# Second MLP matrix by seven block products per group, with the hidden features kept in memory

## The chip, the cores and the metric

The kernel runs on one core of one Trainium2 chip. The metric is the device time of one execution in microseconds, the median over several runs. TensorE (PE in the profile) multiplies, VectorE (DVE), ScalarE (ACT) and GpSimd (POOL) work on elements, SyncE (SP) issues the transfers.

## The reference

One step of a two-layer backbone over 1024 latent and 256 context tokens, model width 1024. Layer 0 mixes tokens by a gated DeltaNet and windowed attention, layer 1 by a recurrent block; after each mixer comes an MLP with a hidden width of 4096:

```python
def sq_relu_mlp(h, w1, w2):
    return jnp.square(jax.nn.relu(h @ w1)) @ w2
```

Its input is a modulated RMS norm of the residual `x`; its output times a gate (one column for latent, one for context tokens) is added to `x`. All is in float32.

## The kernel before

Everything is kept transposed: features on the 128 partitions, tokens along the free axis, in three token tiles `TT`: two of 512 latent tokens and one of 256 context tokens (the prompt), `ti` = 0, 1, 2. For products of float32 accuracy each operand is split into a rounded part `hi` and a remainder `lo` (type float32r), and three products are summed in PSUM: hi x hi, hi x lo, lo x hi (`gemm_tile`, L466 to L468).

`wload` brings a weight block of 128 x 1024 in two transfers of 256 KB through the raw buffers `wraw` (L451); ScalarE rounds (`whi`, L453), GpSimd or VectorE subtracts (`wlo`, L457). There are four slots of such pairs and four raw buffers.

`ff` is the MLP. The hidden width is cut into 32 chunks of 128. `ff1` computes chunks: 8 input blocks x 3 products for each token tile into a PSUM bank of tag `mm`; ScalarE takes the ReLU (L498) and the rounded square (L499), VectorE the exact square (L501), GpSimd the remainder (L502), into `hidh` and `hidl` (three buffers each). `ff2` multiplies two chunks by their rows of the second matrix: for each of 8 output blocks `o` and each token tile, 2 x 3 products (L518 to L520) into a bank of tag `w`, and VectorE adds bank x gate to the residual tile (L521). There are four banks of each tag. The two alternate, chunk pair by chunk pair, so a chunk lives in SBUF only.

In the last pair the order is token tile by token tile, and `after(o, ti)` is called behind each accumulation. In layer 0 this feeds the next norm (class `Norm`, driven by `norm_steps`): a square on ScalarE for each `o` (L396), its sums over the partitions on TensorE (L332), then per token tile `stat` (sums, L403, power, diagonal rows) and `apply` (L418 to L427), which writes the next `hhi` and `hlo`. What is left over for the last token tile is run inside the first projection of the recurrent mixer (`project` in `mix1`), whose softplus ends at L859 and whose gates multiply at L813. In layer 1 `after` sends finished blocks to the output (L673). Scratch of the norms comes from the MLP's own buffers (`ff_scratch`).

In layer 0's mixer, before the MLP, the memory tensor `dn` carries blocks from one stage (L1444, L1495) to another (L1559).

The Tile framework sets the order on each engine's queue, starting from program order, with a model of the instructions' durations, and derives all waits; buffers with one tag rotate, `bufs` of them. All transfers are issued by SP's queue. `hhi`, `hlo` are the tags `hh0` to `hh2` and `hl0` to `hl2` of the pool `hp`.

## Time and profile before

| | us |
|---|---|
| median of 3 runs | 3313.18 |
| lowest, highest | 3306.25, 3314.08 |
| the profiled execution | 3308.6 |
| its span | 3306.8 |

The span goes from the first to the last recorded instruction. Durations of instructions are from the one profiled execution; matmuls are pipelined, so the recorded durations of neighbours overlap. `PEld` is TensorE's weight load, which runs beside its products. "Idle before" is time for which an engine stood still before an instruction, with what ended it behind the arrow.

### The profile page before, as it was taken

Reading aid. Unit: us, or ns where it says so; the run is one execution under the profiler, and the core shown is the slowest. Engines: PE = TensorE matmul, PEld = TensorE weight load, DVE = VectorE, ACT = ScalarE, POOL = GpSimd, SP = SyncE. Lnnn points to the kernel's source line nnn. Section 1 sums busy time; section 2 is a strip of 40 time slices with the busy share of each in tenths; the row PEclk is TensorE's granted clock in tenths of the full one; section 3 lists DMA queues with packets and bytes.
Section 4 is the critical chain, followed back from the end, with each engine's and each line's share of the span. In section 5 each row is a group of like instructions: output and inputs, shape, how many; then the busy total and the mean of one; then the engine's idle time right before and its main releaser. Section 6 shows DMA issues by size and latency. Waiting matters only on the chain.

```text
span 3306.8 us, 50448 instructions
## 1 busy us (share of the span) xinstructions
PE 3150.0 (95%) x20311; PEld 2555.8 (77%) x20311; DVE 1783.5 (54%) x3080; ACT 1117.5 (34%) x2004; POOL 714.3 (22%) x637
## 2 busy tenths in 40 slices
PE   8989966899999999999999999998999999999999
PEld 5867754665568788888888877886778888888888
DVE  5549887667633544444444447778164444444444
ACT  5455523453332321212121236787142121212121
POOL 0000004455432321212121211000142222222220
PEclk9999987999999999999999999999999999999999
DMA  5356777446951011101010121111211111111111
GB/s 201 86 144 171 182 182 207 127 125 212 285 195 33 32 39 32 45 32 45 33 45 32 45 74 41 40 36 43 82 39 45 39 42 36 41 36 40 38 39 70
DMA packets 219272, 273.90 MB, mean 83 GB/s; under 512 B 71578, under 2 KB 125626, under 8 KB 219038
## 3 DMA queue, kind: packets, MB, share of 16 engines
q1 hardware_dynamic: 219038, 270.68, 27.2%
q8 instruction: 159, 2.61, 0.3%
q14 instruction: 75, 0.61, 0.1%
HBM read 223.69 MB, written 46.92 MB: 82 GB/s over the span
## 4 chain that ended last, share of the span: by engine, by line
PE 76%; DVE 8%; DMA 3%; ACT 3%; issue 2%; POOL 1%; SPq 1%; DVEq 0%; ACTq 0%; POOLq 0%
PE ps_mm L466 13%; PE ps_mm L467 13%; PE ps_mm L468 13%; PE ps_w L518 9%; PE ps_w L519 9%; PE ps_w L520 9%; DVE prod L1473 2%; PE ps_ad L300 2%; PE ps_w L1832 1%; PE ps_w L1828 1%; PE ps_w L332 1%; DVE Vinv L1474 1%; DMA adaw<-ada 1%; PE ps_w L1604 1%; PE ps_s L1791 1%
## 5 line engine op out<-in xcount | busy, mean ns | idle before, releaser
L466 PE MATMUL ps_mm<-hhi,whi 128*128 128x512 f32 (+2 forms) x2768 | 991.1, 359 | 21.0 <-ACT hhi L564 13.5
L467 PE MATMUL ps_mm<-hlo,whi 128*128 128x512 f32 (+2 forms) x2768 | 990.1, 358 | 11.0 <-POOL hlo L427 10.8
L468 PE MATMUL ps_mm<-hhi,wlo 128*128 128x512 f32 (+2 forms) x2768 | 987.8, 358 | 0.7 <-POOL wlo L457 0.7
L521 DVE SCALAR_TENSOR_TENSOR x<-ps_w,mod,x 128x512 f32<-128x512 f32 (+1 forms) x768 | 504.1, 660 | 590.9 <-PE ps_w L520 590.9
L466 PEld LDWEIGHTS ps_mm<-hhi,whi 128*128 128x128 f32 (+1 forms) x2768 | 525.8, 190 | 105.2 <-ACT hhi L564 13.9
L467 PEld LDWEIGHTS ps_mm<-hlo,whi 128*128 128x128 f32 (+1 forms) x2768 | 526.0, 190 | 92.9 <-POOL hlo L427 14.3
L468 PEld LDWEIGHTS ps_mm<-hhi,wlo 128*128 128x128 f32 (+1 forms) x2768 | 526.2, 190 | 79.8 <-issue 6.4
L519 PE MATMUL ps_w<-hidl,whi 128*128 128x512 f32 (+1 forms) x1536 | 546.5, 356 | 1.7 <-POOL hidl L502 1.7
L518 PE MATMUL ps_w<-hidh,whi 128*128 128x512 f32 (+1 forms) x1536 | 545.8, 355 | 0.0
L520 PE MATMUL ps_w<-hidh,wlo 128*128 128x512 f32 (+1 forms) x1536 | 543.8, 354 | 0.0
L502 POOL TENSOR_TENSOR hidl<-ffs,hidh 128x512 fp32r<-128x512 f32 (+1 forms) x192 | 226.5, 1180 | 1217.4 <-ACT hidh L499 977.8
L498 ACT ACTIVATE ffr<-ps_mm 128x512 f32<-128x512 f32 (+1 forms) x192 | 100.4, 523 | 902.7 <-PE ps_mm L468 883.6
L453 ACT CAST whi<-wraw 128x512 fp32r<-128x512 f32 x365 | 211.8, 617 | 516.4 <-PE ps_w L519 301.0
L501 DVE TENSOR_TENSOR ffs<-ffr 128x512 f32<-128x512 f32 (+1 forms) x192 | 164.3, 855 | 331.6 <-ACT ffr L498 327.9
L518 PEld LDWEIGHTS ps_w<-hidh,whi 128*128 128x128 f32 x1536 | 290.5, 189 | 45.7 <-issue 1.4
L519 PEld LDWEIGHTS ps_w<-hidl,whi 128*128 128x128 f32 x1536 | 290.4, 189 | 45.0 <-POOL hidl L502 2.5
L520 PEld LDWEIGHTS ps_w<-hidh,wlo 128*128 128x128 f32 x1536 | 289.7, 189 | 41.9 <-issue 0.6
L457 POOL TENSOR_TENSOR wlo<-wraw,whi 128x512 fp32r<-128x512 f32 (+1 forms) x157 | 210.4, 1361 | 259.7 <-ACT whi L453 157.7
L457 DVE TENSOR_TENSOR wlo<-wraw,whi 128x512 fp32r<-128x512 f32 x208 | 147.8, 733 | 90.9 <-ACT whi L453 90.8
L499 ACT ACTIVATE hidh<-ffr 128x512 fp32r<-128x512 f32 (+1 forms) x192 | 107.4, 560 | 5.8
L580 DVE SCALAR_TENSOR_TENSOR x<-ps_mm,mod,x 128x512 f32<-128x512 f32 (+1 forms) x40 | 25.9, 655 | 149.0 <-PE ps_mm L468 138.5
L300 PE MATMUL ps_ad<-adaw,sc 128*32 128x512 f32 x320 | 81.7, 653 | 18.8 <-DMA adaw<-ada 18.8
(377 smaller groups left out, 3272.4 us busy)
## 6 DMA issues: line engine op xcount, KB each, us to landing
wraw<-ff SPq DMA_DIRECT2D x256, 256.0 KB
adaw<-ada SPq DMA_DIRECT2D x80, 512.0 KB
wraw<-w_in SPq DMA_DIRECT2D x76, 256.0 KB
dn<-NI SPq DMA_DIRECT2D x40, 256.0 KB
aw<-ada SPq DMA_DIRECT2D x16, 512.0 KB
wraw<-w_out SPq DMA_DIRECT2D x32, 256.0 KB
dkv<-tok SPq DMA_DIRECT2D x20, 256.0 KB
rtab<-rope SPq DMA_DIRECT2D x10, 512.0 KB
```

What stands on the lines that cost most here:

```text
L300: nc.tensor.matmul(ps[32 * j:32 * j + 32, :], g.sc[:, k, :], w[:, i, :], start=k == 0, stop=k == KC - 1, skip_group_check=True)
L453: nc.scalar.copy(hv[:, o:o + half], raw[:, :half])
L457: e.tensor_tensor(lv[:, o:o + half], raw[:, :half], hv[:, o:o + half], op=ALU.subtract)
L466: nc.tensor.matmul(ps, whi[:, k, :], hhi[:, k, :], start=first and k == k0, stop=False)
L467: nc.tensor.matmul(ps, whi[:, k, :], hlo[:, k, :], start=False, stop=False)
L468: nc.tensor.matmul(ps, wlo[:, k, :], hhi[:, k, :], start=False, stop=last and k == k1 - 1)
L501: nc.vector.tensor_tensor(s[:, :tw], r[:, :tw], r[:, :tw], op=ALU.mult)
L502: nc.gpsimd.tensor_tensor(hl[:, t0:t0 + tw], s[:, :tw], hh[:, t0:t0 + tw], op=ALU.subtract)
L518: nc.tensor.matmul(ps[:, :tw], whi[:, o, :], hh[:, t0:t0 + tw], start=f == 0, stop=False)
L519: nc.tensor.matmul(ps[:, :tw], whi[:, o, :], hl[:, t0:t0 + tw], start=False, stop=False)
L520: nc.tensor.matmul(ps[:, :tw], wlo[:, o, :], hh[:, t0:t0 + tw], start=False, stop=f == 1)
L521: nc.vector.scalar_tensor_tensor(xt[ti][:, o, :], ps[:, :tw], Gt[:, o, cc:cc + 1], xt[ti][:, o, :], op0=ALU.mult, op1=ALU.add)
```

## The change

`ff` now runs the whole first matrix, then the whole second. `ff1` goes through 16 pairs of chunks, squares on VectorE into one float32 tile `hid` per chunk, forms four differences of feature blocks on GpSimd (`tt`), and writes `hid` and `tt` to the memory tensors `Dh` and `Dt`.

`ff2` goes through 8 groups of 4 chunks. For the latent tokens a group is a 2 x 2 block product: output halves of 512 features, contraction halves of 256 (even and odd chunks), token halves of 512. It is computed by Strassen's scheme in Winograd's form: seven block products instead of eight, with sums and differences of weight blocks (GpSimd, on the raw weights) and of feature blocks (read from `Dt`). Each block product is 4 banks x 2 chunks x 3 products; a chain of four of them stays in the same four `mm` banks, and VectorE adds the running bank to the residual after each step where the scheme wants it. The prompt is multiplied in the plain way, from the weight blocks that are there anyway. Raw weights (`ar`), raw features (`br`) and the prompt's split features (`pp`) take over the buffers of `hhi` and `hlo`; feature sets are split by ScalarE and VectorE into `tt` and `hid` in turn, weight sets by ScalarE and GpSimd.

Because the last group finishes the token tiles in the order 0, 2, 1, `norm_steps` and the first `project` take this order. In `mix1` the scratch of the softplus moves into a slice of an `rr` buffer.

The diff; the removed body of `ff` and empty lines are left out (the old body is among the functions printed above):

```diff
@@ -389,8 +389,8 @@
             self.flush(k - 1)
         else:
             self.ps = bank(self.g, SUMTAG)
-        if k == KC - 1 and self.ti == 2:
-            self.sq = self.g.cp.tile([128, self.tw], F32, tag="nsq", name="nsq", bufs=1)
+        if k == KC - 1 and self.late:
+            self.sq = self.g.cp.tile([128, 512], F32, tag="nsq", name="nsq", bufs=1)[:, :self.tw]
         else:
             self.sq = self.al("t%d" % (k % 2))[:, :self.tw]
         self.g.nc.scalar.activation(self.sq, self.x[:, k, :], AF.Square)
...
+NG = NFC // 4
 def ff(g, l, xt, hhi, hlo, Gt, pend, after):
...
+    Dh = g.dp.tile([NFC // 2, 128, 2, T], F32, name=f"dh{l}")
+    Dt = g.dp.tile([NFC // 2, 128, 4, 512], F32, name=f"dt{l}")
+    ff1(g, l, hhi, hlo, pend, Dh, Dt)
+    ff2(g, l, xt, Gt, after, Dh, Dt)
+def ff1(g, l, hhi, hlo, pend, Dh, Dt):
+    nc, pool = g.nc, g.fp
+    for p in range(NFC // 2):
+        ws = [wload(g, g.A["ff1"][l, 2 * p + i], lo_eng=("pool", "dve")[i]) for i in range(2)]
+        hid = [pool.tile([128, T], F32, tag="hid", name="hid", bufs=4) for i in range(2)]
         for ti, (t0, tw) in enumerate(TT):
+            for i in range(2):
                 ps = bank(g, "mm")
+                gemm_tile(g, ps[:, :tw], *ws[i], hhi[ti], hlo[ti])
+                if pend and i:
                     pend.pop(0)()
                 r = pool.tile([128, 512], F32, tag="ffr", name="ffr", bufs=2)
                 nc.scalar.activation(r[:, :tw], ps[:, :tw], AF.Relu)
+                nc.vector.tensor_tensor(hid[i][:, t0:t0 + tw], r[:, :tw], r[:, :tw], op=ALU.mult)
+        t = pool.tile([128, 4, 512], F32, tag="tt", name="tt", bufs=2)
+        (b11, b12), (b21, b22) = [[h[:, 0:512], h[:, 512:1024]] for h in hid]
+        for j, (x, y) in enumerate(((b12, b11), (b22, t[:, 0]), (b22, b12), (b21, t[:, 1]))):
+            nc.gpsimd.tensor_tensor(t[:, j], x, y, op=ALU.subtract)
+        for i in range(2):
+            nc.sync.dma_start(Dh[p, :, i], hid[i])
+        nc.sync.dma_start(Dt[p], t)
+def ff2(g, l, xt, Gt, after, Dh, Dt):
+    nc, pool, src = g.nc, g.fp, g.A["ff2"][l]
+    count = [0]
+    def acc(ps, ti, o):
+        cc, tw = (0, 0, 1)[ti], TT[ti][1]
+        nc.vector.scalar_tensor_tensor(xt[ti][:, o, :], ps[:, :tw], Gt[:, o, cc:cc + 1], xt[ti][:, o, :], op0=ALU.mult, op1=ALU.add)
+    def weights(srcs):
+        w, i = g.wslots[g.nw % len(g.wslots)]
+        g.nw += 1
+        hi, lo = [w.tile([128, KC, 128], F32R, tag=n + str(i), name=n).rearrange("p k c -> p (k c)") for n in ("whi", "wlo")]
+        n = 1024 // len(srcs)
+        for j, s in enumerate(srcs):
+            c = slice(n * j, n * j + n)
+            nc.scalar.copy(hi[:, c], s)
+            nc.gpsimd.tensor_tensor(lo[:, c], s, hi[:, c], op=ALU.subtract)
+        return hi, lo
+    def split(raw, hi, lo):
+        nc.scalar.copy(hi, raw)
+        nc.vector.tensor_tensor(lo, raw, hi, op=ALU.subtract)
+        return hi, lo
+    def three(ps, a, b, first, last):
+        (ah, al), (bh, bl) = a, b
+        nc.tensor.matmul(ps, ah, bh, start=first, stop=False, skip_group_check=True)
+        nc.tensor.matmul(ps, ah, bl, start=False, stop=False, skip_group_check=True)
+        nc.tensor.matmul(ps, al, bh, start=False, stop=last, skip_group_check=True)
+    def product(pss, a, b, m, first):
+        for i in range(2):
+            c, t = slice(512 * i + 128 * m, 512 * i + 128 * m + 128), slice(512 * i, 512 * i + 512)
+            three(pss[m], [v[:, c] for v in a], [v[:, t] for v in b], first and i == 0, i == 1)
+    for gi in range(NG):
+        last, q = gi == NG - 1, gi % 2
+        ar = g.hp.tile([128, 4, 1024], F32, tag=f"hh{q}", name="ar", bufs=1)
+        br = g.hp.tile([128, 4, 1024], F32, tag=f"hl{q}", name="br", bufs=1)
+        pp = g.hp.tile([128, 2, 1024], F32R, tag=("hh2", "hl2")[q], name="pp", bufs=1)
+        nbr = [0]
+        def load_w(b):
+            for i in range(2):
+                nc.sync.dma_start(ar[:, b, 512 * i:512 * i + 512], src[4 * gi + 2 * i + b % 2][:, 512 * (b // 2):512 * (b // 2) + 512])
+        def feats(srcs):
+            raw = br[:, nbr[0] % 4]
+            nbr[0] += 1
+            for i, s in enumerate(srcs):
+                nc.sync.dma_start(raw[:, 512 * i:512 * i + 512], s)
+            count[0] += 1
+            if count[0] % 2:
+                t = pool.tile([128, 2, 1024], F32R, tag="tt", name="bb", bufs=2)
+                return split(raw, t[:, 0], t[:, 1])
+            return split(raw, *[pool.tile([128, 1024], F32R, tag="hid", name="b" + n, bufs=4) for n in "hl"])
+        def block_of(i, ti):
+            return [Dh[2 * gi + j, :, i, 512 * ti:512 * ti + 512] for j in range(2)]
+        def comb(j):
+            return [Dt[2 * gi + i, :, j - 1] for i in range(2)]
+        def prompt(ws, o0):
+            for m in range(4):
+                ps = bank(g, "w")[:, :256]
+                for i in range(2):
+                    for c in range(2):
+                        w = slice(512 * i + 128 * m, 512 * i + 128 * m + 128)
+                        f = 256 * (2 * i + c)
+                        three(ps, [v[:, w] for v in ws[c]], [pp[:, x, f:f + 256] for x in range(2)], i + c == 0, i + c == 2)
+                acc(ps, 2, o0 + m)
+        chain = [bank(g, "mm") for m in range(4)]
+        load_w(0)
+        a11, b11 = weights([ar[:, 0]]), feats(block_of(0, 0))
+        for m in range(4):
+            product(chain, a11, b11, m, True)
+            acc(chain[m], 0, m)
+        load_w(1)
+        a12, b21 = weights([ar[:, 1]]), feats(block_of(1, 0))
+        pss = [None] * 4
+        for m in range(4):
+            pss[m] = bank(g, "w")
+            product(pss, a12, b21, m, True)
+            acc(pss[m], 0, m)
+        praw = br[:, nbr[0] % 4]
+        nbr[0] += 1
+        for i in range(2):
+            nc.sync.dma_start(praw[:, 512 * i:512 * i + 512].rearrange("p (c t) -> p c t", t=256), Dh[2 * gi + i, :, :, 1024:])
+        split(praw, pp[:, 0], pp[:, 1])
+        prompt((a11, a12), 0)
+        load_w(2)
+        load_w(3)
+        s1, s2 = [[wraw(g) for i in range(2)] for _ in range(2)]
+        for i in range(2):
+            c = slice(512 * i, 512 * i + 512)
+            nc.gpsimd.tensor_tensor(s1[i], ar[:, 2, c], ar[:, 3, c], op=ALU.add)
+            nc.gpsimd.tensor_tensor(s2[i], s1[i], ar[:, 0, c], op=ALU.subtract)
+        w, f = weights(s2), feats(comb(2))
+        for m in range(4):
+            product(chain, w, f, m, False)
+            acc(chain[m], 1, m)
+        nc.gpsimd.tensor_tensor(ar[:, 0], ar[:, 0], ar[:, 2], op=ALU.subtract)
+        w, f = weights([ar[:, 0]]), feats(comb(3))
+        for m in range(4):
+            product(chain, w, f, m, False)
+            acc(chain[m], 1, 4 + m)
+        a22, f = weights([ar[:, 3]]), feats(comb(4))
+        for m in range(4):
+            product(chain, a22, f, m, False)
+            acc(chain[m], 0, 4 + m)
+            if last:
+                after(m, 0)
+        prompt((weights([ar[:, 2]]), a22), 4)
+        w, f = weights(s1), feats(comb(1))
+        for m in range(4):
+            pss[m] = bank(g, "mm" if last else "w")
+            product(pss, w, f, m, True)
+            acc(pss[m], 1, 4 + m)
+            if last:
+                after(4 + m, 0)
+        for i in range(2):
+            c = slice(512 * i, 512 * i + 512)
+            nc.gpsimd.tensor_tensor(ar[:, 1, c], ar[:, 1, c], s2[i], op=ALU.subtract)
+        w, f = weights([ar[:, 1]]), feats(block_of(1, 1))
+        for m in range(4):
+            if last:
+                after(2 * m, 2)
+                after(2 * m + 1, 2)
+            product(pss, w, f, m, False)
+            acc(pss[m], 1, m)
+            if last:
+                after(m, 1)
         if last:
+            for m in range(4):
+                after(4 + m, 1)
...
 def ff_scratch(g):
     def al(tag):
         if tag == "dg":
-            return g.fp.tile([128, T], F32R, tag="hidl", name="ndg", bufs=3)
-        return g.fp.tile([128, 512], F32, tag={"t0": "ffr", "t1": "ffs"}[tag], name="n" + tag, bufs=2)
+            return g.fp.tile([128, T], F32R, tag="hid", name="ndg", bufs=4)
+        return g.fp.tile([128, 512], F32, tag={"t0": "ffr", "t1": "tt"}[tag], name="n" + tag, bufs=2)
     return al
-def norm_steps(g, ab, al, stat_at, apply_at):
+def norm_steps(g, ab, al, stat_at, apply_at, seq=(0, 1, 2)):
     n, h = {}, {}
     def after(o, ti, x):
+        i = seq.index(ti)
         if o == 0:
             n[ti] = Norm(g, ti, x, al)
+            n[ti].late = i == 2
         n[ti].square(o)
-        if ti and o == stat_at[ti]:
-            n[ti - 1].stat()
-        if ti and o == apply_at[ti]:
-            if ti == 1:
+        if i and o == stat_at[i]:
+            n[seq[i - 1]].stat()
+        if i and o == apply_at[i]:
+            if i == 1:
                 h["h"] = htiles(g.hp)
-            n[ti - 1].apply(*ab, *h["h"])
+            n[seq[i - 1]].apply(*ab, *h["h"])
     def late(f):
         def run(al=None):
-            n[2].al = al or n[2].al
+            n[seq[2]].al = al or n[seq[2]].al
             f()
         return run
-    left = [late(lambda: n[2].stat()), late(lambda: n[2].apply(*ab, *h["h"]))]
+    left = [late(lambda: n[seq[2]].stat()), late(lambda: n[seq[2]].apply(*ab, *h["h"]))]
     return after, left, h
@@ -674,7 +799,7 @@
         with ExitStack() as e2:
             ff_pools(g, e2, ("fp", "wx"))
-            step, left, h1 = norm_steps(g, ab, ff_scratch(g), {1: 2, 2: 3}, {1: 5, 2: 7})
+            step, left, h1 = norm_steps(g, ab, ff_scratch(g), {1: 2, 2: 3}, {1: 5, 2: 7}, (0, 2, 1))
             def end0(o, ti, x):
                 step(o, ti, x)
@@ -758,7 +883,8 @@
     def project(jobs):
         ws = [wload(g, A["w_in1"][c], lo_eng="dve") for c, _ in jobs]
-        for ti, (t0, tw) in enumerate(TT):
+        for ti in (0, 2, 1) if left else (0, 1, 2):
+            tw = TT[ti][1]
             for (c, evac), (whi, wlo) in zip(jobs, ws):
                 ps = bank(g, "mm")[:, :tw]
                 gemm_tile(g, ps, whi, wlo, hhi[ti], hlo[ti])
@@ -850,10 +976,11 @@
         return KC + c, evac
     project([xjob(0), gjob(0)])
-    sp = pool.tile([128, 16], F32, name="sp")
-    nlam = pool.tile([128, 16], F32, name="nlam")
+    tp = Slices([full("rr", 2)])
+    sp = tp.tile([128, 16], F32)
+    nlam = tp.tile([128, 16], F32)
     nc.vector.tensor_scalar(nlam, g.par["lam"], -1.0, None, op0=ALU.mult)
-    softplus(g, sp, nlam, pool, "lsp")
+    softplus(g, sp, nlam, tp, "lsp")
     m8, p4 = pool.tile([128, 16], F32, name="m8"), pool.tile([128, 16], F32, name="p4")
     nc.vector.tensor_scalar(m8, sp, -8.0, None, op0=ALU.mult)
     nc.vector.tensor_scalar(p4, sp, 4.0, None, op0=ALU.mult)
```

## Rows read from the trace of the kernel before

**Rows 1.** the page: busy us, share, instructions; TensorE and its clock in 40 slices

```profile
PE 3150.0 (95%) x20311; PEld 2555.8 (77%) x20311; DVE 1783.5 (54%) x3080; ACT 1117.5 (34%) x2004; POOL 714.3 (22%) x637
...
PE   8989966899999999999999999998999999999999
...
PEclk9999987999999999999999999999999999999999
```

**Rows 2.** the page: the chain that ended last, shares of the span by line

```profile
PE ps_mm L466 13%; PE ps_mm L467 13%; PE ps_mm L468 13%; PE ps_w L518 9%; PE ps_w L519 9%; PE ps_w L520 9%; DVE prod L1473 2%; PE ps_ad L300 2%; PE ps_w L1832 1%; PE ps_w L1828 1%; PE ps_w L332 1%; DVE Vinv L1474 1%; DMA adaw<-ada 1%; PE ps_w L1604 1%; PE ps_s L1791 1%
```

**Rows 3.** windows, inside the first MLP and in a DMA-heavy stretch before it

```profile
core 0: us, PE busy (x) PEld busy (x) DVE busy (x) ACT busy (x) POOL busy (x), PEclk, DMA share, GB/s
1120.00:1900.00 780.00, 780.00 (x4066) 671.14 (x4065) 331.36 (x480) 149.28 (x282) 175.34 (x143) 1.00 0.12 39
800.00:900.00 100.00, 95.84 (x1343) 55.61 (x1341) 74.13 (x188) 39.20 (x102) 54.73 (x45) 1.00 0.85 246
```

**Rows 4.** groups by form, 1120 to 1900: count, busy, mean ns, idle before

```profile
L518 PE MATMUL ps_w<-hidh,whi 128*128 128x512 f32 x455 | 178.2, 392 | 0.0
...
L521 DVE SCALAR_TENSOR_TENSOR x<-ps_w,mod,x 128x512 f32<-128x512 f32 x227 | 170.1, 750 | 207.5 <-PE ps_w L520 207.5
...
L453 ACT CAST whi<-wraw 128x512 fp32r<-128x512 f32 x114 | 66.1, 617 | 203.9 <-PE ps_w L519 139.8 <-DMA wraw<-ff 38.2 <-PE ps_mm L467 22.8
...
L521 DVE SCALAR_TENSOR_TENSOR x<-ps_w,mod,x 128x256 f32<-128x256 f32 x113 | 54.5, 482 | 53.4 <-PE ps_w L520 53.4
```

**Rows 5.** timeline of TensorE, runs of equal products: start us, us, instruction

```profile
1059.03 0.28 PE L466 MATMUL ps_mm<-hhi,whi 128*128 128x256 f32 x1
...
1062.15 0.28 PE L468 MATMUL ps_mm<-hhi,wlo 128*128 128x256 f32 x1
...
1065.24 0.39 PE L466 MATMUL ps_mm<-hhi,whi 128*128 128x512 f32 x1
...
1067.51 0.39 PE L467 MATMUL ps_mm<-hlo,whi 128*128 128x512 f32 x1
```

**Rows 6.** timeline of VectorE, first MLP

```profile
1317.07 1.28 DVE L457 TENSOR_TENSOR wlo<-wraw,whi 128x512 fp32r<-128x512 f32 x2
...
1338.14 0.75 DVE L521 SCALAR_TENSOR_TENSOR x<-ps_w,mod,x 128x512 f32<-128x512 f32 x1 [2.87 <-PE ps_w L520]
1338.81 1.40 DVE L501 TENSOR_TENSOR ffs<-ffr 128x256 f32<-128x256 f32 x1
```

**Rows 7.** timeline of GpSimd, the same stretch

```profile
1337.37 2.55 POOL L457 TENSOR_TENSOR wlo<-wraw,whi 128x512 fp32r<-128x512 f32 x2 [0.66 <-ACT whi L453]
```

**Rows 8.** weight loads, SP's queue: ns min/median/max, first and last start

```profile
L451 SPq DMA_DIRECT2D wraw<-ff x256: 327/328/914, 987.3 to 3271.2; - x128
```

**Rows 9.** the chain in order of time: a 512 KB load

```profile
753.44 4.90 DMA adaw<-ada
```

**Rows 10.** the memory tensor `dn`: ns min/median/max, first and last start

```profile
L1559 SPq DMA_DIRECT2D XW<-dn x40: 444/476/1499, 475.5 to 875.9; - x40
...
L1495 SPq DMA_DIRECT2D dn<-VB x20: 500/616/801, 337.4 to 555.1; - x20
```

**Rows 11.** timeline of VectorE from the first MLP into the recurrent mixer

```profile
1956.36 0.15 DVE L403 TENSOR_SCALAR nst<-ps_w 128x4 f32<-128x4 f32 x1
...
2008.95 0.17 DVE L859 TENSOR_SCALAR p<-sp 128x16 f32<-128x16 f32 x1
```

**Rows 12.** timeline of TensorE, the same stretch

```profile
1965.06 0.73 PE L466 MATMUL ps_mm<-hhi,whi 128*128 128x512 f32 x2 [0.43 <-ACT hhi L419]
...
2017.76 1.09 PE L813 MATMUL ps_w<-xh,lwhi 128*128 128x512 f32 x4
```

**Rows 13.** windows: ten us of it

```profile
1990.00:2000.00 10.00, 7.56 (x20) 5.69 (x21) 9.64 (x13) 6.42 (x11) 6.19 (x7) 0.66 0.17 52
```

**Rows 14.** timeline of VectorE, the last accumulation

```profile
3303.33 0.48 DVE L521 SCALAR_TENSOR_TENSOR x<-ps_w,mod,x 128x256 f32<-128x256 f32 x1 [0.23 <-PE ps_w L520]
```

More of the change, by code (lines that the diff above doesn't have):

```diff
@@ L526, in ff @@
-    ff1(0, 1)
-    for gi in range(NFC // 2):
-        c0 = 2 * gi
-        if c0 + 2 < NFC:
-            ff1(c0 + 2)
-        ff2(c0)
-        if c0 + 3 < NFC:
-            ff1(c0 + 3)
-        del hid[c0], hid[c0 + 1], w2[c0], w2[c0 + 1]
+                nc.vector.tensor_tensor(hid[i][:, t0:t0 + tw], r[:, :tw], r[:, :tw], op=ALU.mult)
[3 more added lines that the diff above has]
+            nc.gpsimd.tensor_tensor(t[:, j], x, y, op=ALU.subtract)
```

36 lines of the change are left out of this document (removed).

## The prediction

> **What bounds the kernel now.** I read the page's busy shares first: TensorE is busy for 95% of the span, VectorE for 54%, GpSimd for 22% [rows 1]. An average says little over a kernel with two mixers and two MLPs, so next comes the chain that ended last, by line: L466 to L468 (the first MLP matrix and every other dense product that goes through `gemm_tile`) and L518 to L520 (the second MLP matrix) hold 66% of it [rows 2]. Then the stretch in the middle of the first MLP: in 780 us TensorE has no idle time at all and its granted clock is 1.00, while DMA works at 39 GB/s and GpSimd for 175 us [rows 3]. Both MLPs are TensorE-bound to the last instruction. There a matmul that is not issued is time saved, as long as nobody else becomes late.
>
> What is one matmul worth? Not its modelled duration of 392 ns [rows 4], since matmuls overlap; it is the distance of two starts. In a row of 128x512 products ten steps take 2.27 us: 0.227 us each. In a row of 128x256 products 26 steps take 3.12 us: 0.12 us each [rows 5]. So a pair of hidden chunks costs 192 x 0.227 + 96 x 0.12 = 55.1 us for both matrices, half of it, 27.5 us, in the second.
>
> **The matmuls.** Before, 4 hidden chunks take 4 x 8 x 2 x 3 = 192 products 512 wide and 96 products 256 wide in the second matrix. After, a group of 4 chunks takes 7 block products of 4 x 2 x 3 = 24, so 168, and the prompt again 2 x 48 = 96. That is 24 fewer x 8 groups x 2 layers = 384 x 0.227 = **-87.1 us**. A group now lasts 168 x 0.227 + 96 x 0.12 = 49.6 us, a block product 5.45 us. The first matrix keeps its 27.5 us for a pair.
>
> **Who must keep up in 49.6 us.** VectorE: 28 accumulations at 0.750 and 8 at 0.482 [rows 4] make 24.9 us; eight feature sets (seven blocks and the prompt) are split anew, and one of 1024 columns is like two of 512, 1.28 us [rows 6], so 10.2; 35.1 in all. GpSimd: a 1024-wide subtraction is two of 512, 2.55 us [rows 7]. Eight weight sets make 20.4; the sums and differences of weights add another four times 1024 columns, 10.2; 30.6 in all. ScalarE rounds 16 sets of 1024 at about 1.2 (two of 0.617 [rows 4]): 20 us. SP issues 8 weight and 16 feature transfers at 0.33 us [rows 8], 8 us. Memory: 24 x 256 KB is 6.3 MB in 49.6 us, 127 GB/s; in the first matrix, 3.4 MB a pair in 27.5 us, 124 GB/s. The trace carries 246 GB/s in another stage [rows 3]. So each of them fits with a margin, and these edits cost nothing under TensorE's 49.6 us. Buffers give the distance: a feature set's destination comes free three block products before it is needed, a weight slot at least two (11 us), and a chain of load, rounding and remainder is 4.9 (half a megabyte, [rows 9]) + 1.2 + 2.6 = 8.7 us.
>
> **The wait that the change adds.** VectorE and GpSimd do not run as freely side by side as this sum pretends. GpSimd worked from 1337.37 to 1339.92; VectorE's 256-wide product of two SBUF operands that began at 1338.81 took 1.40 us and ended 0.29 us after GpSimd [rows 6, 7]. It waited. The accumulation at 1338.14, one operand in PSUM, took its usual 0.75 in the same time [rows 6]. So the splits wait for GpSimd, the accumulations do not, but they stand behind the splits in VectorE's queue, and TensorE waits for their banks. The Trainium skill, SBUF — State Buffer, section "Who interferes with whom", has it as a rule that speaks against this change: a read and write port pair of SBUF is locked exclusively, for a whole instruction, between GpSimd and VectorE instructions with two SBUF inputs; the trace agrees, with the 1.40 us. By the Trainium skill's rule the lock would be held 30.6 + 10.2 = 40.8 of 49.6 us, which still fits.
>
> Now the price. Bounds for one split's wait: nothing, or one whole GpSimd instruction, 2.55 us. GpSimd is busy 62% of the group, so 0.62 x 1.3 = 0.8 us on average: 6.4 us a group, and VectorE stands at 41.5 of 49.6. A bank is wanted again after three quarters of a product, 4.1 us after its last matmul, and its accumulation needs 0.75: 3.3 us of slack against at most 1.28 + 2.55 = 3.8. Only the worst of 128 splits reach TensorE, with half a microsecond each: I take **+5**, bounds 0 and 20.
>
> **From the first matrix to the second** nothing overlaps any more by two chunk halves. The raw buffers take over `hh0` and `hl0`, which are free after the last pair's first token half, so 48 x 0.227 + 48 x 0.12 = 16.6 us before the first matrix ends, against the 8.7 us chain. Would the read of the features wait for the last write to the same memory tensor? No: the first read of `dn` starts at 475.5 while the last write of that tensor starts far later (its writes at L1495 run to 555.1) [rows 10]; overlap goes by region. **+2** for both layers, bounds 0 and 10.
>
> **The end of layer 0.** The next norm's first half needs all eight squares, and odd ones use the slots of `tt`, which the last feature sets also use; the eighth gets its slot when the block product before the last is done, 5.45 us before TensorE runs out. From the sums to the first product of the next stage the trace has 8.7 us (1956.36 to 1965.06) [rows 11, 12], and I allow 3 us, an estimate from the same stretch, for the square, its sums and their copy ahead of it: 11.7 - 5.5 = 6 us late. Before, prompt products of the last pair filled this; now they are finished earlier. And the clock falls to half (1.2 of 2.4 GHz) for some time after such a gap: in 1990 to 2000, granted 0.66 on average, 20 products took 10 us where 4.5 would do [rows 13]. The second and third parts had such gaps already, and some of the 6 us goes to what TensorE still has to do of the norm. **+6**, bounds 0 (sums hoisted) and 18 (three gaps of 6 us). The recurrent mixer's other edits cost nothing: its token parts change places, and the softplus works in slices of an `rr` buffer, which the gates need; before, it was done at 2009.1 and the first gate product began at 2017.8 [rows 11, 12]. Without those 8.6 us of air it would be late by as much, once.
>
> **The tail.** The last transfer is now 512 KB, not 256; before, 3.0 us lie between the last accumulation's end and the end of the span [rows 14]. The 512 KB of [rows 9] took 4.9. **+2.5**, bounds 0 and 5.
>
> **The sum.** The profiled execution took 3308.6 us (span 3306.8 and 1.8 around it): 3308.6 - 87.1 + 5 + 2 + 6 + 2.5 = 3237. It lies 4.6 us under the median of the runs; I place the time between, at **3239**. All lower bounds together give 3221.5, all upper ones 3274.
>
> **The rivals.** (a) *Part of the gain is eaten by late accumulations.* If the fixed order of the queues does not foresee these waits and each of the 128 splits stalls TensorE for 0.4 us, that is +51, so 3284 (the case reaches from 3274 to 3303). For it: VectorE has 8 us of air in 49.6 by my average. Against: a bank's 3.3 us of slack. 0.12. (b) *VectorE becomes the bound, and the kernel is slower.* If every split waits for a whole GpSimd instruction, a group is 24.9 + 10.2 + 8 x 2.55 = 55.5 us of VectorE, 5.9 more than TensorE has; 16 groups make +94, so 3308.6 - 87.1 + 94 + 10 = 3326. It decides over TensorE from 1.8 us of wait a split, and the kernel is slower from 2.4. It is the lock of the Trainium skill's SBUF — State Buffer, taken at its worst. Against it: GpSimd idles 38% of the time. 0.08. (c) *Memory.* If transfers reached only 110 GB/s, a group would be 57 us; 3308.6 - 87.1 + 16 x 7.6 + 10 = 3353. Nothing in the trace at a high DMA share is that slow. 0.03. (d) *The gain is lost in sum,* (a) at 0.6 us a split: 3308, no change. 0.05.
>
> **Chances.** The forecast, within its bounds of 3221 to 3274, has 0.72. Faster is the forecast and (a): 0.84. Within 0.3%, which is 10 us and about what the runs' own spread can tell: 0.05. Slower, (b) and (c): 0.11. For 8 in 10 the range goes from 3221 into the middle of (a), 3285.
>
> **What would show it.** Right: 2688 products 512 wide in the second matrix in place of 3072; TensorE without idle inside the groups, 49.6 us apart; the first matrix at 27.5 us a pair. The lock: splits well over 1.3 us next to GpSimd's subtractions, and, if (a) or (b), TensorE idle until a VectorE accumulation. The seam at layer 0's end: TensorE idle for some 5 us before the projection, and a granted clock under 1. Wrong: a group well over 49.6 us, or TensorE waiting for weights.

## The result and the profile after

The kernel after the change takes 3234.8 us (median of 4 runs, 3231.9 to 3240.2), the one before 3313.6 on the same chip (4 runs, 3306.3 to 3317.0): a ratio of 0.9767, 95% interval 0.9746 to 0.9788, or 78.8 us. The profiled execution took 3233.9 us, its span 3232.1. The forecast was 3239, its range 3221 to 3285.

The page of after, with the lines that answer to [rows 1]: busy time, then TensorE and its granted clock in 40 slices.

```profile
PE 3060.8 (95%) x19927; PEld 2485.3 (77%) x19927; DVE 1864.1 (58%) x2952; ACT 1209.4 (37%) x1972; POOL 1117.5 (35%) x781
...
PE   8989975889989999999999998999899999999999
...
PEclk9999986999999999999999998999999999999999
```

TensorE lost 89.2 us of busy time and kept its 95%: it is still the bound, and all others got busier (GpSimd from 714 to 1118 us). Windows of after inside the first MLP: the seam between the two matrices, then a stretch of the second matrix (columns as in [rows 3]).

```profile
1520.00:1540.00 20.00, 19.83 (x117) 17.35 (x116) 16.78 (x14) 6.84 (x9) 19.53 (x12) 1.00 0.93 329
1540.00:1560.00 20.00, 17.99 (x93) 15.47 (x94) 17.72 (x21) 8.11 (x10) 19.76 (x11) 1.00 0.64 229
...
1600.00:1650.00 50.00, 50.00 (x268) 43.33 (x268) 37.04 (x45) 16.32 (x18) 33.44 (x19) 1.00 0.39 127
```

In the groups TensorE has no idle time, at a granted clock of 1.00, with VectorE at 37 of 50 us, GpSimd at 33 and DMA at 127 GB/s. The same work stands once in each group, for instance the remainder of the prompt's features; timeline of VectorE in after:

```profile
1616.76 1.64 DVE L541 TENSOR_TENSOR pp<-br,pp 128x1024 fp32r<-128x1024 f32 x1 [0.41 <-ACT pp L540]
...
1815.47 1.65 DVE L541 TENSOR_TENSOR pp<-br,pp 128x1024 fp32r<-128x1024 f32 x1 [0.40 <-ACT pp L540]
```

Four groups take 198.71 us, 49.68 each; the forecast was 49.6. Only the seam is different: there GpSimd is busy for 39.3 of 40 us, and TensorE is missing 2.2. The view of waits of after, TensorE, from the start of layer 0's MLP to the end; its five largest lines:

```profile
PE ps_mm L466 <- ACT hhi L686: 13.5, 2, 13.0
PE ps_mm L466 <- ACT hhi L419: 9.7, 7, 1.6
PE ps_mm L467 <- POOL hlo L427: 8.8, 5, 2.3
PE ps_w L368 <- DVE ndg L361: 6.5, 5, 2.5
PE ps_w L546 <- DVE x L526: 4.6, 2, 2.4
```

The last line is the second matrix: two waits in all (us, times, longest), one at each layer's seam. The others are seams of norms and projections. Before waits there too, but less: the same view of it sums to 38.0 us, this one to 45.5, and waits for the row spread of a norm (L368, 6.5 us) have no line in it. The 13.0 us ahead of layer 1's first projection are in both.

**What a comparison can resolve.** Between before and after, 7 us of span go to a stretch that the change leaves alone. From the first projection after layer 0's mixer (its first product that waits for a remainder on VectorE: 938.81 us in before, 945.89 in after) to the end of the span it is 3306.8 - 938.81 = 2368.0 us before and 3232.1 - 945.89 = 2286.2 after: -81.8 where the spans differ by -74.7. I call this *the stretch from layer 0's projection*, and the experiments are compared in it too.

### The profile page after: what moved, and what is told of

The parts are those of the page before. It is cut to its first block, busy times and chain, and to the rows that moved or that the text cites. A ratio compares the mean times of both kernels' runs of the same rounds, so it can differ in the third digit from the quotient of the medians.

```text
span 3232.1 us, 50272 instructions
## 1 busy us (share of the span) xinstructions
PE 3060.8 (95%) x19927; PEld 2485.3 (77%) x19927; DVE 1864.1 (58%) x2952; ACT 1209.4 (37%) x1972; POOL 1117.5 (35%) x781
## 4 chain that ended last, share of the span: by engine, by line
PE 74%; DVE 8%; DMA 3%; issue 3%; ACT 2%; POOL 2%; SPq 1%; DVEq 0%; POOLq 0%; ACTq 0%
PE ps_mm L467 14%; PE ps_mm L466 14%; PE ps_mm L468 13%; PE ps_w L546 4%; PE ps_w L547 4%; PE ps_w L548 4%; PE ps_mm L547 4%; PE ps_mm L548 4%; PE ps_mm L546 4%; DVE prod L1600 2%; PE ps_ad L300 2%; PE ps_w L1959 1%; DVE Vinv L1601 1%; PE ps_w L1955 1%; PE ps_s L1918 1%
## 5 line engine op out<-in xcount | busy, mean ns | idle before, releaser
L468 PEld LDWEIGHTS ps_mm<-hhi,wlo 128*128 128x128 f32 (+1 forms) x2768 | 526.3, 190 | 81.8 <-issue 6.0
L507 DVE TENSOR_TENSOR hid<-ffr 128x512 f32<-128x512 f32 (+1 forms) x192 | 148.9, 777 | 589.3 <-ACT ffr L506 507.1
L536 POOL TENSOR_TENSOR wlo<-ar,whi 128x1024 fp32r<-128x1024 f32 x96 | 246.7, 2584 | 268.7 <-ACT whi L535 251.2
L526 DVE SCALAR_TENSOR_TENSOR x<-ps_mm,mod,x 128x512 f32<-128x512 f32 x272 | 200.4, 746 | 82.8 <-PE ps_mm L548 82.6
L526 DVE SCALAR_TENSOR_TENSOR x<-ps_w,mod,x 128x512 f32<-128x512 f32 (+1 forms) x304 | 185.6, 632 | 100.7 <-PE ps_w L548 100.5
L511 POOL TENSOR_TENSOR tt<-hid 128x512 f32<-128x512 f32 x64 | 83.3, 1301 | 414.0 <-DVE hid L507 414.0
L453 ACT CAST whi<-wraw 128x512 fp32r<-128x512 f32 (+1 forms) x237 | 136.7, 617 | 197.9 <-PE ps_mm L467 84.1
L535 ACT CAST whi<-ar 128x1024 fp32r<-128x1024 f32 x96 | 98.0, 1051 | 292.6 <-PE ps_w L547 208.3
L546 PE MATMUL ps_w<-pp,whi 128*128 128x256 f32 x512 | 143.6, 283 | 4.6 <-DVE x L526 4.6
L547 PE MATMUL ps_w<-pp,whi 128*128 128x256 f32 x512 | 143.4, 283 | 0.0
L548 PE MATMUL ps_w<-pp,wlo 128*128 128x256 f32 x512 | 141.0, 283 | 0.0
L511 POOL TENSOR_TENSOR tt<-hid,tt 128x512 f32<-128x512 f32 x64 | 85.3, 1333 | 118.2 <-DVE hid L507 118.0
```

Of the source, the lines that this page charges most:

```text
L453: nc.scalar.copy(hv[:, o:o + half], raw[:, :half])
L468: nc.tensor.matmul(ps, wlo[:, k, :], hhi[:, k, :], start=False, stop=last and k == k1 - 1)
L507: nc.vector.tensor_tensor(hid[i][:, t0:t0 + tw], r[:, :tw], r[:, :tw], op=ALU.mult)
L511: nc.gpsimd.tensor_tensor(t[:, j], x, y, op=ALU.subtract)
L526: nc.vector.scalar_tensor_tensor(xt[ti][:, o, :], ps[:, :tw], Gt[:, o, cc:cc + 1], xt[ti][:, o, :], op0=ALU.mult, op1=ALU.add)
L536: nc.gpsimd.tensor_tensor(lo[:, c], s, hi[:, c], op=ALU.subtract)
```

## The experiments

**An eighth product.** In every group a11 x b11 is issued twice into the same banks; the second overwrites the first.

```diff
             product(chain, a11, b11, m, True)
+            product(chain, a11, b11, m, True)
```

> The first block product of each group is issued twice (the second start overwrites the first, so all else is as in the changed kernel): 24 more products of 512 columns in each of 16 groups. Theory (TensorE sets the pace of every group, the gain is the product that is left out): 384 x 0.227 = 87 us more, 3322 us, a little over the kernel before. Rival (the gain comes from running the two matrices one after the other, with fewer accumulations and one split each, and TensorE has air): less than half of it, under 3280.

Measured: 3324.9 us, ratio to before 1.0028 (1.0017 to 1.0039), 90.1 us over after. The 384 products cost what their distance says, 87.1, and a little more. TensorE sets the time, and the products are the gain: with the eighth one the changed kernel is 0.28% slower than the one before, so the rest of the change wins nothing by itself.

**Six products.** s2 x c2 is left out, its sets are still loaded and split.

```diff
         w, f = weights(s2), feats(comb(2))
         for m in range(4):
-            product(chain, w, f, m, False)
```

> The products of the second weight combination are left out (24 in each group; its weights and features are still loaded and split, its accumulations still done, the values are not the scheme's). Theory: VectorE, GpSimd and memory have air, so 87 us less, 3148. Rival (the lock between VectorE and GpSimd is the next bound, just under TensorE): a group of 44 us meets late accumulations, only 40 to 65 us less, and TensorE waits for accumulations inside the groups.

Measured: 3174.5 us, ratio 0.9568 (0.9547 to 0.9588): 60 us under after, not 87, the rival's size. The groups nearly keep up; the view of waits, TensorE, layer 0's second matrix, its largest line:

```profile
PE ps_mm L548 <- POOL wlo L536: 5.3, 2, 4.8
```

Late accumulations inside the groups, the rival's mechanism, are not what it shows (0.2 us). Here a late remainder of weights (L536, GpSimd) makes TensorE wait for 4.8 us at the seam, and the clock granted in 1560 to 1600 is 0.92. In the groups, the prompt's remainders stand 44.70 us apart, not 49.68 - 5.45 = 44.23. So with one product less TensorE is no longer alone in setting the pace: 0.47 us a group goes to others, and more at the seams; from the start of layer 0's MLP on, the view of waits sums to 59.5 us, 14 more than in after. Whether that is GpSimd was tried further below.

**Without the lock.** The features' remainder is a ScalarE copy in place of VectorE's subtraction.

```diff
-        nc.vector.tensor_tensor(lo, raw, hi, op=ALU.subtract)
+        nc.scalar.copy(lo, raw)
```

> The remainder of each feature set is replaced by a plain copy on ScalarE (the subtraction is left out, values change), so VectorE has no instruction with two SBUF operands in the second matrix and cannot wait for GpSimd. Theory (the lock reaches TensorE only at the seam of the two matrices, 2.2 and 2.4 us of waiting for accumulations): 4 to 6 us less, 3230. Rival (late accumulations cost inside the groups too): over 12 us less.

Measured: 3229.3 us, ratio 0.9735 (0.9717 to 0.9753), 5.4 us under after as the theory said; no wait for an accumulation is left at either seam. What the lock does is seen in durations. Groups by form of after, 1600 to 1900 us (count, busy us, mean ns, idle before):

```profile
L526 DVE SCALAR_TENSOR_TENSOR x<-ps_mm,mod,x 128x512 f32<-128x512 f32 x97 | 71.9, 746 | 29.5 <-PE ps_mm L548 29.5
...
L541 DVE TENSOR_TENSOR bb<-br,bb 128x1024 fp32r<-128x1024 f32 x20 | 34.1, 1703 | 3.7 <-ACT bb L540 3.7
...
L536 POOL TENSOR_TENSOR wlo<-wraw,whi 128x512 fp32r<-128x512 f32 x26 | 40.0, 1561 | 0.0
```

And of the kernel without VectorE's subtractions:

```profile
L526 DVE SCALAR_TENSOR_TENSOR x<-ps_mm,mod,x 128x512 f32<-128x512 f32 x97 | 72.8, 750 | 58.3 <-PE ps_mm L548 58.3
...
L536 POOL TENSOR_TENSOR wlo<-wraw,whi 128x512 fp32r<-128x512 f32 x24 | 30.7, 1302 | 0.0
```

GpSimd's 512-wide instructions take 1.30 us in the run without the splits. Beside the splits three of their four groups take 1.56 to 1.86 on average, and one (L617) stays at 1.30. A split takes 1.65 to 1.77 on average, against 1.24 for one that is not held up (at 1540.05 us, shown below). An accumulation, with one operand in PSUM, takes 0.75 in both.

**The features' memory read twice.** Every feature transfer of the second matrix is issued twice; the prompt's features are not touched.

```diff
             for i, s in enumerate(srcs):
                 nc.sync.dma_start(raw[:, 512 * i:512 * i + 512], s)
+                nc.sync.dma_start(raw[:, 512 * i:512 * i + 512], s)
```

> Every feature block of the second matrix is read from memory twice into the same place: 3.7 MB more in each group of 49.6 us, about 200 GB/s instead of 127. Theory (the way through memory is hidden): no change, within 5 us. Rival (transfers are near their limit): 30 us or more, with ScalarE's rounding waiting for transfers and TensorE for it.

Measured: 3237.5 us, ratio 0.9765 (0.9744 to 0.9786): no difference that the runs can tell. Its window of 1600 to 1650 us shows 200 GB/s in place of 127 and TensorE at 50.00 of 50.

Memory is hidden with room to spare; the rival of memory falls.

**Weights' remainders on VectorE, and features' remainders on GpSimd.** One call of the second matrix moved, each way.

```diff
-            nc.gpsimd.tensor_tensor(lo[:, c], s, hi[:, c], op=ALU.subtract)
+            nc.vector.tensor_tensor(lo[:, c], s, hi[:, c], op=ALU.subtract)
```

> The remainders of the second matrix's weights are worked out by VectorE in place of GpSimd. VectorE then has 24.9 + 10.2 + 10.2 = 45.3 us of work in a group of 49.6, GpSimd only the 10.2 us of sums and differences; the lock between the two gets rare. If the lock at its measured size is what costs VectorE time (0.5 us a split at 62% of GpSimd), its waits fall to some 0.1 us each, VectorE ends at 47 of 49.6 and TensorE is held up now and then: 3235 to 3250. Rival, VectorE's plain load being the bound before its average says so: groups longer than 51 us, over 3260.

Measured: 3231.7 us, ratio 0.9752 (0.9736 to 0.9767), under both expectations. VectorE as the bound is refuted at 45 of 50 us; a window of this run:

```profile
1600.00:1650.00 50.00, 50.00 (x269) 43.41 (x268) 44.90 (x56) 16.30 (x18) 14.75 (x8) 1.00 0.37 127
```

TensorE's waits for accumulations fell from 4.6 to 1.8 us, the 3 us by which the median is lower, though the intervals overlap. Here VectorE carries 8 us more than in after and TensorE waits less: what hurt was the two engines' getting in each other's way at the seam, not VectorE's load. GpSimd has less to do here as well; in the run without the lock it had the same instructions as in after, and the waits were gone all the same.

```diff
-        nc.vector.tensor_tensor(lo, raw, hi, op=ALU.subtract)
+        nc.gpsimd.tensor_tensor(lo, raw, hi, op=ALU.subtract)
```

> The remainders of the features are worked out by GpSimd in place of VectorE. GpSimd then has 30.6 + 8 x 2.55 = 51.0 us of work in a group for which TensorE needs 49.6; VectorE has no operation with two SBUF operands left in the second matrix, so that the lock can't matter there. If GpSimd's durations are fixed (2.55 us a 1024-wide subtraction), it is the bound: at least 1.4 x 16 = 23 us slower than after, 3258, with waits of its chain up to 3300; TensorE waits for GpSimd. Rival: GpSimd's own durations hold waits for VectorE too; free of the lock it fits, and the time stays at 3228 to 3240.

Measured: 3248.8 us, ratio 0.9813 (0.9789 to 0.9837), 14 us over after, between the two expectations, and both had a part wrong. The seam of this run:

```profile
1540.00:1560.00 20.00, 14.25 (x75) 12.03 (x74) 5.38 (x9) 4.85 (x6) 20.00 (x11) 0.91 0.10 31
```

Free of the lock GpSimd needs 2.44 us for a 1024-wide subtraction, not 2.55; the load fits, at 48.33 of 50 in 1800 to 1850 us, once the backlog of the seam is worked off, and TensorE runs through. The loss is at the seams, where it waits 5.1 and 5.0 us for a weight's remainder and the clock falls to 0.91.

**The slots of the norm's odd squares.** The prediction named a `tt` slot as the reason for the idle time at the end of layer 0.

```diff
-        return g.fp.tile([128, 512], F32, tag={"t0": "ffr", "t1": "tt"}[tag], name="n" + tag, bufs=2)
+        return g.fp.tile([128, 512], F32, tag={"t0": "ffr", "t1": "ffr"}[tag], name="n" + tag, bufs=2)
```

> The odd squares of the norm go to the slots of `ffr` in place of those of `tt`; nothing else is touched. The prediction said that the eighth square of the next norm waits for a `tt` slot until the block product before the last, and that this makes the 5 us of TensorE's idle time ahead of layer 0's next projection. If so, the sums of the eighth square come a product earlier and the time falls by 4 to 6 us, to 3229 to 3231. Rival: in the profile of after the eighth square is done at about 1922.7 us, 6 us before TensorE runs out, and its sums and their transpose stand in TensorE's queue behind (nearly) all products of the last block: then the slot is not what is late, and the time stays within 1.5 us of after's 3235.

Measured: 3261.5 us, ratio 0.9845 (0.983 to 0.986): 26.7 slower than after, which neither theory foresaw. The edit hits every norm around the MLPs. In 1060 to 1140 us, the start of layer 0's MLP, TensorE waits 13.4 us, where after waits 5.9; at the start of layer 1's it is 13.1 against 5.5. So 15 of the 26.7 us are waits at the two MLP starts. The granted clock is lower there too, 0.91 against 0.96 in 1060 to 1140 and 0.91 against 0.97 in 2360 to 2460, which is at most 10 us more. With every norm changed the run can't be read for the end of layer 0. The edit was made again there alone:

```diff
-        if k == KC - 1 and self.late:
+        if k == KC - 1 and self.late or k % 2 and self.own:
...
+            n[ti].own = i == 0 and seq[1] == 2
```

> Only at the end of layer 0, and only for the first token part, the odd squares of the next norm go to a tile of their own (`nsq`) in place of the slots of `tt`; no other norm is touched, so what hurt where odd squares shared the slots of `ffr` is gone. Theory that the place in TensorE's queue sets the 5 us idle time: no change against after, 3233 to 3237. Rival, the prediction's slot of `tt`: the sums come a block product earlier, 3228 to 3231.

Measured: 3240.8 us, ratio 0.9786 (0.9771 to 0.98), 6 over after and over both ranges. Its timeline of TensorE at the end of layer 0:

```profile
1934.97 0.42 PE L332 MATMUL ps_w<-nsq,con 128*32 128x128 f32 x8
...
1943.24 1.22 PE L466 MATMUL ps_mm<-hhi,whi 128*128 128x512 f32 x2 [1.60 <-ACT hhi L419]
```

ScalarE had finished the eighth square, now in its own tile, at 1930.3; its sums came 4.7 us later, and the three waits (1.85 for the row spread, 1.60, and 1.78 for the first remainder) are those of after. The slot was not what was late. As for the time, this profile's first remainder product of layer 0's projection comes at 951.65 us, 5.8 later than in after's, in instructions ahead of the edit; from there to the end it is 3242.6 - 951.65 = 2290.9 us, a length that the unedited kernel shows too (2290.7, below).

**The norm's first part one product earlier.** Its squares, and the prompt's with the first part's statistics, are issued in the last group one product earlier.

```diff
             acc(chain[m], 1, 4 + m)
+            if last:
+                after(m, 0)
...
             if last:
-                after(m, 0)
+                after(4 + m, 0)
...
             if last:
-                after(4 + m, 0)
+                after(m, 2)
...
             if last:
-                after(2 * m, 2)
-                after(2 * m + 1, 2)
+                after(4 + m, 2)
             product(pss, w, f, m, False)
```

> In the last group of an MLP the squares of the next norm's first part are issued with the third and fourth of the latent features' products in place of the fifth and sixth (their x is complete there), and the prompt's squares, with the first part's statistics among them, with the last but one product. The same instructions, one product (5.45 us) earlier. If the place in the queue makes the idle time, the whole statistics and row spread stand ahead of the last product, the first projection product follows TensorE's last block product within 1 us, and the time falls by 5 to 7 us (the 5.1 us from the norm's statistics to the first projection product, and up to 2 us of clock given back), to 3228 to 3230. Rival: the chain is bound by ScalarE and VectorE (hhi, hlo of the first part), which the earlier place doesn't shorten, or the sums' bank is missed by the last prompt products: a gain under 2 us, or a loss of the same size.

Measured: 3232.0 us, ratio 0.9752 (0.9737 to 0.9766): 2.7 under after, less than expected. TensorE at the end of layer 0 in after:

```profile
1928.38 0.40 PE L548 MATMUL ps_mm<-bh,wlo 128*128 128x512 f32 x1
1928.71 1.07 PE L332 MATMUL ps_w<-nt,con 128*32 128x128 f32 x24
1929.76 0.33 PE L347 MATMUL ps_w<-con,nt 128*128 128x128 f32 x1
...
1932.65 0.50 PE L368 MATMUL ps_w<-ndg,onesr 128*128 128x512 f32 x1 [1.86 <-DVE ndg L361]
...
1935.27 1.22 PE L466 MATMUL ps_mm<-hhi,whi 128*128 128x512 f32 x2 [1.59 <-ACT hhi L419]
```

And with the norm earlier:

```profile
1920.59 0.33 PE L347 MATMUL ps_w<-con,nt 128*128 128x128 f32 x1
...
1924.29 0.79 PE L368 MATMUL ps_w<-ndg,onesr 128*128 128x512 f32 x1 [1.59 <-DVE ndg L361]
...
1927.44 0.63 PE L548 MATMUL ps_mm<-bh,wlo 128*128 128x512 f32 x1
1927.87 0.63 PE L546 MATMUL ps_mm<-bh,whi 128*128 128x512 f32 x1
...
1932.83 0.39 PE L548 MATMUL ps_mm<-bh,wlo 128*128 128x512 f32 x1
1933.15 0.43 PE L332 MATMUL ps_w<-nt,con 128*32 128x128 f32 x8
1933.50 0.73 PE L466 MATMUL ps_mm<-hhi,whi 128*128 128x512 f32 x2
```

The transpose of the sums (L347) stood behind the last block product, and now stands ahead of it; the first projection product follows without a wait, and 0.49 us are lost at its first remainder, where the three waits (with 1.79 for that remainder) took 5.2. So the place in TensorE's queue made this idle time. The gain is smaller, since there are still waits ahead of the row spread (1.59 here, and 0.74 for two squares): in all TensorE waits 11.8 us at the end of layer 0, for 14.0 in after. And the clock falls: 0.50 in 1924 to 1930 us, the lower of the two levels, with 14 matmuls in 6 us, 0.43 us each. From layer 0's projection to the third part's first remainder product (1968.89 - 942.28) it is 1026.6 us, in after (1975.18 - 945.89) 1029.3 and in a second profile of after (below) 1030.5. To the end of the span it is 3230.5 - 942.28 = 2288.2, between the 2286.2 and 2290.7 of those two, so the gain shows at its place and not in the whole.

**Both helps together.**

> The norm's first part one product earlier, and the remainders of the second matrix's weights on VectorE: the two edits that won 2.7 and 3.0 us apart. The first ends an idle time at the end of layer 0, the second one at the start of the second matrix, which don't touch each other: they add to 5.7, 3229, with TensorE's waits on accumulations under 2 us and no wait ahead of the first projection product of over 2 us. Rival: VectorE, busy for 45 of 50 us in a group, is late for the norm's earlier statistics in the last group, and the sum stays at 3232.

Measured: 3233.5 us, ratio 0.9768 (0.9754 to 0.9781), 1.3 under after and so no better that the runs can tell. By the profile the two do add in part: TensorE's waits on accumulations are 1.7 us, and layer 0's projection to the third part's first remainder product is 1025.4 us. But this projection begins at 945.99, as late as in after, and the time of the run has that in it. A gain of 5 us is not resolved.

**Six products with the weights on VectorE.** The edits of the second and the fifth run.

> The products of s2 with c2 are left out, as in the run with six products, and the weights' remainders are worked out by VectorE. Theory: what six products lost of their 87 us (they won 60) was GpSimd's burst at the start of the second matrix, through late remainders of weights and the lock; with GpSimd relieved the whole 87 us come back: 3148 +- 5. Rival: VectorE, 39 to 42 us of 44.1, or the loads are the next limit, and it stays at 3165 to 3185.

Measured: 3179.2 us, ratio 0.9605 (0.9592 to 0.9619): the rival. In 1600 to 1650 us GpSimd is busy for 13.0 us and VectorE for 47.2 of 50; a group takes 45.67 us, and TensorE waits 11.4 us in 15 waits for rounded weights (ScalarE) and 8.4 us at the seams for accumulations. So GpSimd's burst was not the only thing that six products ran into; relieving it only moved the waits, and a split of the work between the two engines wasn't tried.

**The changed kernel once more.**

> The changed kernel once more, unedited. In the profiles so far the first projection after layer 0's mixer, in instructions that the change does not touch and that stand in the same order, begins anywhere from 938.8 to 951.7 us. Theory: this is the run's own variation, ahead of the change, and the 7.1 us of it that the first profile of after shows against before are no cost of the change. Then the start of that projection lies elsewhere again (not at 945.9), and the time from there to the end of the span is the same within 2 us as in the first profile, 2286 (2284 to 2288), with TensorE waiting 4 to 6 us for accumulations at the start of the second matrices. Rival: the 7 us belong to the changed program (its memory tensors or its code lie elsewhere), and the projection starts at 945.9 +- 1 again.

Measured: 3237.0 us, ratio 0.9765 (0.975 to 0.978). The first remainder product of layer 0's projection, in the first profile of after:

```profile
945.89 0.50 PE L467 MATMUL ps_w<-hlo,whi 128*128 128x512 f32 x1 [1.93 <-DVE hlo L687]
```

And in the second, of the same kernel:

```profile
939.60 0.80 PE L467 MATMUL ps_w<-hlo,whi 128*128 128x512 f32 x1 [2.51 <-DVE hlo L687]
```

So the 7.1 us are no cost of the change: the mixer ahead of it varies by itself. The second half of the expectation fails: the stretch from there to the end is 3230.3 - 939.6 = 2290.7 us, 4.5 longer than in the first profile. It is not the waits, which sum to 48.6 us from 940 us on, for 50.4 in the first. It is mostly the granted clock. Windows of the first profile, at the third part of layer 0's projection and at the seam of layer 1:

```profile
1971.00:1981.00 10.00, 7.04 (x22) 5.18 (x23) 9.76 (x15) 7.14 (x12) 5.44 (x4) 0.66 0.00 0
2840.00:2850.00 10.00, 7.56 (x53) 6.79 (x53) 8.21 (x9) 4.24 (x5) 9.43 (x6) 1.00 1.03 399
```

The same places in the second:

```profile
1966.00:1976.00 10.00, 7.17 (x16) 5.20 (x17) 9.76 (x15) 7.14 (x12) 5.57 (x4) 0.50 0.00 0
2840.00:2850.00 10.00, 8.08 (x39) 6.95 (x38) 7.16 (x9) 5.23 (x6) 9.51 (x5) 0.83 0.80 310
```

In the ten us from the projection's remainder product on it is 0.83 in the first and 0.71 in the second. Together that is 1.6 + 1.7 + 1.2 = 4.5 us of clock, as an estimate and an upper one, since TensorE was at work for 70 to 94% of these windows. Gains of 2 to 5 us, as of the edits above, are within what the same kernel shows twice; I take them as read from waits that vanish, not from times.

## Why the prediction was right, step by step

**The matmuls (-87.1).** The mechanism was right, the size 4 us short. The page's groups of after hold 6 x 272 + 6 x 176 = 2688 products 512 wide in the second matrix, 384 fewer; a group takes 49.68 us for 49.6. A pair of chunks of the first matrix takes 27.54 for 27.5; GpSimd in after, the same work in two pairs:

```profile
1155.46 1.29 POOL L511 TENSOR_TENSOR tt<-hid 128x512 f32<-128x512 f32 x1 [15.10 <-DVE hid L507]
...
1183.00 1.29 POOL L511 TENSOR_TENSOR tt<-hid 128x512 f32<-128x512 f32 x1 [15.10 <-DVE hid L507]
```

But before, a pair took 55.24 us for both matrices, where the forecast added up 55.1; VectorE in before:

```profile
1300.36 0.75 DVE L521 SCALAR_TENSOR_TENSOR x<-ps_w,mod,x 128x512 f32<-128x512 f32 x1 [1.36 <-PE ps_w L520]
...
1355.60 0.75 DVE L521 SCALAR_TENSOR_TENSOR x<-ps_w,mod,x 128x512 f32<-128x512 f32 x1 [1.36 <-PE ps_w L520]
```

So a pair fell from 55.24 to 27.54 + 49.68 / 2 = 52.38 us, and the 32 pairs of the two layers make 91.5 us. The eighth product costs 90.1. (384 x 0.227 is 87.2, not 87.1.)

**Who must keep up.** Right: 37.0 us of VectorE a 50 us window for 35.1 a group of 49.6 before waits, 33.4 of GpSimd in the same window for 30.6 a group, DMA 127 GB/s for 127; doubled feature reads cost nothing that the runs can tell. GpSimd's surplus over the sum is the lock, which lengthens its instructions too, a side that the sum did not have.

**The lock (+5).** The size was near and the place wrong. A split's wait is 0.5 us on average, not 0.8, and not one of 128 splits reaches TensorE inside the groups, so the "worst of 128 splits" failed as a step. The time is lost where GpSimd has no pause at all. VectorE at the seam in after:

```profile
1535.71 3.36 DVE L541 TENSOR_TENSOR bl<-br,bh 128x1024 fp32r<-128x1024 f32 x1
1540.05 1.24 DVE L541 TENSOR_TENSOR pp<-br,pp 128x1024 fp32r<-128x1024 f32 x1 [0.98 <-ACT pp L540]
1541.22 1.91 DVE L526 SCALAR_TENSOR_TENSOR x<-ps_w,mod,x 128x512 f32<-128x512 f32 x4
```

And GpSimd:

```profile
1533.33 2.30 POOL L511 TENSOR_TENSOR tt<-hid,tt 128x512 f32<-128x512 f32 x1
1535.59 2.40 POOL L623 TENSOR_TENSOR ar<-ar 128x1024 f32<-128x1024 f32 x1
1537.95 2.27 POOL L644 TENSOR_TENSOR ar<-ar,wraw 128x512 f32<-128x512 f32 x1
```

The split that begins at 1535.71 waits for L623 and takes 3.36 us; the prompt's split behind it waits another 0.98 for its rounding, which stood in ScalarE's queue behind one that had waited 4.19 us for L623; and four accumulations (one of 512 columns, three of 256), 1.91 us, stand behind both while TensorE waits for their banks, 2.2 us here and 2.4 in layer 1. By the Trainium skill, SBUF — State Buffer, section "Who interferes with whom", GpSimd and a VectorE instruction that needs the shared port pair exclude each other; the trace agrees, and the accumulations' 0.75 us in either run agrees with it too.

**The seam (+2)** is the same 4.6 us, so lock and seam together were 7 in the forecast and 4.6 measured, 4.9 in the second profile; taking the lock away gave 5.4.

**The end of layer 0 (+6).** The picture was right: 5.2 us idle ahead of the projection, for some 5 foretold, and a clock of 0.69 in 1930 to 1940. The working behind it was not. VectorE read the sums at 1930.13:

```profile
1930.13 0.16 DVE L403 TENSOR_SCALAR nst<-ps_w 128x4 f32<-128x4 f32 x1 [0.56 <-PE ps_w L347]
```

The projection's first product came at 1935.27, 5.1 us later, where the forecast took 8.7 from before and 3 more ahead of the sums. And the 5.5 us of head start were not there: the sums and their transpose stood in TensorE's queue behind the last products (moved: the wait is gone), and the `tt` slot named for the eighth square has no part in it (own slot: same waits). Two errors met, and that their difference came to some 5 us is luck.

The size was wrong too. From the last products to the third part TensorE waits 12.5 us in before (1930 to 2030 us):

```profile
PE ps_mm L467 <- POOL hlo L427: 5.8, 3, 2.3
PE ps_w L332 <- ACT nt L396: 3.0, 2, 2.0
PE ps_mm L466 <- ACT hhi L419: 2.9, 3, 1.4
```

And 14.0 in after (1925 to 1982):

```profile
PE ps_mm L467 <- POOL hlo L427: 4.7, 3, 1.8
PE ps_w L368 <- DVE ndg L361: 4.6, 3, 2.5
PE ps_mm L466 <- ACT hhi L419: 4.3, 3, 1.6
```

The net is 1.5 us of waits, since before lost the time at the other parts. The clock adds at most 3.3: it was 0.92 in 1920 to 2025 of before, 8.4 us lost in 105 if TensorE had been at work throughout, and 0.87 in 1900 to 1990 of after, 11.7 in 90. So the cost is 1.5 to 4.8, not 6; the term counted a new gap and not the ones it replaces.

**The tail (+2.5).** From the last accumulation's end (3227.71 + 0.75) to the span's end it is 3.6 us, 3.0 before: +0.6.

**The sum.** By the waits the costs are 4.6 + 1.5 + 0.6 = 6.7. Another 1.6 stand where the forecast had no term, at the starts of the two MLPs: 5.9 and 5.5 us of waits, for 4.9 at each before. Measured against the 91.5 us of gain, the costs are 91.5 - 81.8 = 9.7 by the stretch from layer 0's projection, 14.2 in the second profile, and 91.5 - 78.8 = 12.7 by the medians, for 15.5 in the forecast. So the gain was forecast 4 us too small and the costs some 3 us too large, and that 3239 came within 4.2 us of the median is in part luck. Of the rivals none came near: late accumulations, VectorE and memory fell in the runs above. Open: why the clock was granted differently in two profiles of the same kernel, and what ends the gain with six products.

## What to carry to other kernels

Price a removed matmul by the distance of starts in a full row, and check that every helper engine fits under the shorter period with its waits. The new group's length held here to 0.2%. The saving held only to 5%, since the old period was added up (55.1) where it could be read off the trace (55.24): read both periods where one is there to be read. Look for losses at the ends of the stretch, not in its middle: at a seam two stages' bursts fall together, and an average load says nothing. When a seam moves, compare its idle time, and the clock granted around it, with what it replaces; and when something is late, look first at what stands ahead of it in its engine's queue before a buffer is blamed.

## What the runs showed of the hardware

The exclusion between GpSimd and VectorE costs both: 0.4 to 0.5 us a 1.24 us split and up to 0.56 us a 1.30 us subtraction, at 67% of GpSimd's time busy.

After waits of 0.54, 0.20 and 1.59 us within 4 us, with only the norm's small products between them, TensorE worked at the lower clock for 6 us (14 products at 0.43 us), though in the 780 us before it had been idle for only the seam's 2.9 us. A single wait did not always do that: at the seam of layer 1 the clock stayed at 1.00 after 2.44 us in the first profile of after, and fell (0.83 in 2840 to 2850 us) with a wait of 1.92 in the second.

And after one unchanged stretch the next stage began anywhere from 938.8 to 951.7 us in the profiles of this study, more than the 8.3 us between the fastest and the slowest run of after.
